# A WKV kernel: one row loaded by another engine's queue, six raw tiles in another pool, fewer leading zero matmuls

## Chip, cores and metric

The kernel runs on one core of a Trainium2 chip. The metric is the device time of one execution in microseconds (us), the median of several runs. A profile of one execution goes with it; its times are counted from the start of its span.

Names: PE is TensorE (matmuls; PEld its weight loads), DVE is VectorE, ACT is ScalarE, POOL is GpSimd, SP is SyncE. A "q" behind an engine's name stands for its sequencer, which issues DMAs and waits on semaphores.

## Reference

Inputs are w and u of 256 channels, and k and v of 16 sequences x 2048 steps x 256 channels, all float32. For each sequence and channel the reference runs along t with a weighted sum aa, its weight bb and a running maximum pp that keeps the exponentials in range:

```
ww = u + kk;  qq = max(pp, ww);  e1 = exp(pp - qq);  e2 = exp(ww - qq)
out[t] = (e1 * aa + e2 * vv) / (e1 * bb + e2 + 1e-08)
ww = pp - w + kk;  qq = max(ww, kk);  e1 = exp(ww - qq);  e2 = exp(kk - qq)
aa = e1 * aa + e2 * vv;  bb = e1 * bb + e2;  pp = qq
```

k, v and the output are 33.6 MB each.

## The kernel before, in words

Time is cut into 16 chunks of 128 steps (TC), the 16 sequences into 4 groups of 4. A step n = 4c + p is chunk c and group p, 64 steps in all (NP). A tile of k or v for a step is 128 x 4 x 256 float32, 512 KB: 128 time steps on the partitions, four sequences beside each other.

For a step n, in order:

- LK and LV load k and v (`load_k`, L104, `load_v`, L112). For n < 3 (BYSP) SP issues them, otherwise POOL.
- RK (`round_k`, L191) casts the raw k to fp32r on DVE or POOL. For some steps, 3 to 10 among them, the DMA casts on its way and there is no RK.
- R and L (`rows`, L196, and `logs`, L203), for q = 0 and 1, are the matmuls that make an exponent tile X in PSUM: R spreads the rows of w and u, which lie in the tile WU, over the time steps (L200), L adds sums of k over time (L206). There are two X tiles in turn.
- X (`exps`, L208) is ACT's exponential of an X tile into the ring EZR.
- CV casts v to bf16 (L213), TV multiplies it by the exponentials (L218, DVE).
- S (`sums`, L237) adds up over a chunk (L244). After four steps the state of the chunk is carried on by a chain of small operations on DVE, ACT and PE (`copy_sums` to `copy_back`, L248 to L306; L257 and L301 are its matmuls).
- Ten steps later (LAG) follow DEN, LN, INV, NUM, MUL and ST: denominators and numerators by PE (L321), logarithm and exponential by ACT (L329, L337), the product by DVE (L349) into an output tile of the pool opool, and the stores by SP, some of the last ones by POOL (L355, L362).

The order on all engines is written out by a planner. Each operation has a place (a number from the table P, by step), and the planner takes the first one in order of place whose predecessors are done and whose buffer is free (`free`, L370; NV = 4 raw tiles of vpool, NOT = 8 of opool). So buffers set the order of instructions, and on the chip an instruction that writes a buffer waits until the one before has been read. Each engine and each DMA queue works in its own order.

Zero matmuls on the tile Z (`zeros`, L146 to L148) fill PE's stream at fixed places: 38 at the very start, 12 before the rows of each of the first two X tiles (P["Z0"]["R"]), others later. They compute nothing that is used.

What comes before the first step: the tile WUf is cleared by DVE (L123). ACT issues the loads of w and u into it (`row_wu`, L120), one row of 256 channels each to four partitions. `make_rows` (L173, place "wu") turns it into WU on DVE (L174, L175) after DVE has cast the first k. POOL makes masks by selects (L83) and counts by iotas (L155), out of which DVE makes NLE, NLZ and CO (L159 to L163).

The first three k and v, raw, take tiles of vpool in the order k0, k1, v0, k2, v1, v2, then come v3 and the later v. vpool has four tiles, so v1, v2 and v3 wait until k0, k1 and k2 have been cast. The output tiles of opool are first needed when step 0 is finished.

Of the kernel before, what the change touches and what calls it, by code (L numbers as in the profile page):

```python
# [15 lines left out]
def kernel(  # L16
# [9 lines left out]
    K = tc.keep_in_program_order  # L26
    PE, DVE, SC, POOL, SP = nc.tensor, nc.vector, nc.scalar, nc.gpsimd, nc.sync
# [6 lines left out]
    NP = 4 * NST  # L34
    RING = 11
    LAG = 10.0
    SOON = 0
    UNTIL = 16
    SHARE = 0.2
    BYSP = 3  # L40
# [4 lines left out]
    CAP = 54.0  # L45
    BIG = 1e30
    FIRST = "DDDCCCCCCCC"
    VOT = 0
    XT = 8
    BYPOOL = 52  # L50
    BYQ = "PSSP"
# [16 lines left out]
    kppool = ctx.enter_context(tc.tile_pool(name="kppool", bufs=NKP))  # L68
    vpool = ctx.enter_context(tc.tile_pool(name="vpool", bufs=NV))
    vbpool = ctx.enter_context(tc.tile_pool(name="vbpool", bufs=NVB))  # L70
    rpool = ctx.enter_context(tc.tile_pool(name="rpool", bufs=NRD))
    opool = ctx.enter_context(tc.tile_pool(name="opool", bufs=NOT))
# [19 lines left out]
    def rows_of(x, n):  # L92
        c, p = divmod(n, 4)
        return x[4 * p:4 * p + 4, c * TC:(c + 1) * TC, :].rearrange("n t d -> t n d")

    KR, VR, VB = {}, {}, {}

    def how(n):
        return "D" if n < BYSP else FIRST[n] if n < len(FIRST) else PLAN[n % len(PLAN)]

    def raw(pool, tag):
        return pool.tile([128, 4, Dm], F32, tag=tag, name=tag)

    def load_k(n):  # L104
        if how(n) != "C":
            KR[n] = raw(vpool, "vr") if n < BYSP else raw(kppool, "kf")
            K((SP if n < BYSP else POOL).dma_start(out=KR[n], in_=rows_of(k, n)))  # L107
        else:
            KR[n] = kpool.tile([128, 4, Dm], F32R, tag="kr", name="kr")
            K(POOL.dma_start(out=KR[n], in_=rows_of(k, n)))  # L110

    def load_v(n):  # L112
        vr = raw(opool, "ot") if n < VOT else raw(vpool, "vr")
        K((SP if n < BYSP else POOL).dma_start(out=vr, in_=rows_of(v, n)))  # L114
        VR[n] = vr
# [4 lines left out]
    def row_wu(queue, x, g):  # L120
        K(queue.dma_start(out=WUf[g::32, :], in_=bass.AP(tensor=x.tensor, offset=x.offset, ap=[[0, 4], list(x.ap[0])])))

    K(DVE.memset(WUf, 0.0))  # L123
    load_k(0)
    row_wu(SC, w, 0)
    row_wu(SC, u, 1)
    K(SC.preload_act_table_set("natural_log_exp_and_others"))
    M1, I1 = matrix("M1", F32), matrix("I1", F32)
    K(DVE.memset(M1, -1.0))
# [16 lines left out]
    def zeros(m, first=False):  # L146
        for j in range(m):
            K(PE.matmul(TURN[:, 0:192], Z[:, 0:128], Z, start=first, stop=True, skip_group_check=True))  # L148

    zeros(38, True)  # L150

    select(M1, GE, 0.0, -1, -1, [[1, 128]])
    select(I1, NE, 1.0, 0, -1, [[1, 128]])
# [155 lines left out]
    RD, NUM, OT = {}, {}, {}  # L309
# [29 lines left out]
    def by_x(n):  # L339
        return n >= NP - XT and n % 2 == 1  # L340
# [16 lines left out]
    def shared(n):  # L357
        return n >= BYPOOL or BYQ[n % len(BYQ)] == "P" and n >= BYF
# [11 lines left out]
    ops, free = {}, {"K": NK, "KP": NKP, "V": NV, "N": 1, "RD": NRD, "OT": NOT, "VB": NVB}  # L370

    def step(name, place, fn, args=(), after=(), take=None, give=(), mode=0):
        key = name if isinstance(name, str) else " ".join(map(str, name))
        ops[name] = dict(place=AT.get(key, place), fn=fn, args=args, after=list(after), take=take, give=give, mode=mode)

    for n in range(NP):
        c, j = divmod(n, 4)
        early = n < BYSP
        vb = "OT" if n < VOT else "V"
        put = lambda key: n + P[key][j]  # L380
        lead = SOON * max(0.0, 1 - n / UNTIL)
        m = n + LAG - lead
        tail = n >= NP - LAG
        place = lambda key: m + (P["TAIL"][key] + (n - NP + LAG) * P["TAIL"]["step"] if tail else P["OUT"][key][j])
        kb = "V" if early else "KP" if how(n) != "C" else "K"
        if n:
            step(("LK", n), n + P["LK"], load_k, (n,), [("LK", n - 1)], kb)
        else:
            free["V"] -= 1
        step(("LV", n), n + P["LV"], load_v, (n,), [("LV", n - 1)] + ([("LK", n)] if n else []), vb)  # L390
        if how(n) != "C":
            step(("RK", n), put("RK"), round_k, (n,), [("LK", n), ("RK", n - 1)], "K", [kb])
        for q in range(2):
            step(("R", q, n), n + P["R"][q], rows, (n, q), ["wu", ("R", 1 - q, n - 1 + q)], "X", mode=3)
            step(("L", q, n), n + P["L"][q], logs, (n, q), [("R", q, n), ("LK", n), ("RK", n), ("L", 1 - q, n - 1 + q)], None,
                 ["K"] if q else [], 1)
            step(("X", q, n), n + P["X"][q], exps, (n, q), [("L", q, n), ("NUM", n - RING), ("S", n - RING)], None, ["X"])
        step(("CV", n), put("CV"), cast_v, (n,), [("LV", n), ("CV", n - 1)], "VB", [vb])
        step(("TV", n), put("TV"), times_v, (n,), [("X", 1, n), ("CV", n), ("TV", n - 1)], None, ["VB"])
        step(("S", n), put("S"), sums, (n,), [("TV", n), ("S", n - 1)] + ([("CS", c - 1)] if j == 0 else []), mode=2)  # L400
        if j == 3:
            s = P["STATE"][0 if c == 0 else 2 if c == NST - 1 else 1]
            for i, (name, fn, *after) in enumerate((
                    ("CS", copy_sums, ("S", n)), ("TU", turn, ("CS", c), ("CH", c - 1)), ("SL", state_logs, ("TU", c)),
                    ("FR", state_frames, ("SL", c), ("SN", c - 1)), ("OF", state_offsets, ("FR", c)),
                    ("SW", state_weights, ("OF", c)), ("CH", state_chain, ("SW", c), ("KP", c - 1)),
                    ("SS", state_spread, ("CH", c)), ("TK", turn_back, ("SS", c), "mats"), ("BK", copy_back, ("TK", c)),
                    ("SN", state_next, ("OF", c)), ("KP", state_keep, ("CH", c)))):
                if not (name in ("SN", "KP") and c + 1 == NST):
                    step((name, c), n + s[i] - lead * SHARE, fn, (c,), after, mode=1)  # L410
        step(("DEN", n), place("DEN"), den, (n,), [("BK", c), ("DEN", n - 1), "mats"], "X", mode=3)
        step(("LN", n), place("LN"), log_den, (n,), [("DEN", n), ("INV", n - 1)], "RD", ["X"])
        step(("INV", n), place("INV"), inverse, (n,), [("LN", n)])
        step(("NUM", n), place("NUM"), num, (n,), [("BK", c), ("TV", n), ("NUM", n - 1), "mats"], "X" if by_x(n) else "N", mode=3)
        step(("MUL", n), place("MUL"), mult, (n,), [("NUM", n), ("INV", n), ("MUL", n - 1)], "OT", ["X" if by_x(n) else "N", "RD"])
        step(("ST", n), place("ST"), store, (n,), [("MUL", n), ("ST", n - 1)], None, [] if shared(n) else ["OT"])
        if shared(n):
            step(("SQ", n), place("SQ"), store_rest, (n,), [("ST", n)], None, ["OT"])
# [6 lines left out]
    while todo:  # L425
# [15 lines left out]
        for g in o["give"]:  # L441
            if g == "X":
                x = held[("DEN", name[1]) if name[0] == "LN" else ("NUM", name[1]) if name[0] == "MUL" else ("R",) + name[1:]]
# [39 lines left out]
```

## Time and profile before

| | us |
|---|---|
| runs shown, median (lowest to highest) | 292.77 (292.13 to 294.27) |
| the profiled execution, its own time | 293.15 |
| its span | 291.4 |
| PE busy, TensorE's matmuls | 273.7 (94%) |
| ACT busy | 258.4 (89%) |
| DVE busy | 247.1 (85%) |
| POOL busy | 175.7 (60%) |
| DMA, HBM read and written | 345 GB/s over the span |

The granted TensorE clock over the profiled execution is 0.992 of full speed.

How to read it: a line of the timeline is start, length, engine, line of the kernel, operation, tile written <- tiles read, shapes, count, and in brackets the idle time of that engine before it and who ended it. A line of the chain of waits is start, length and what the chain passes through; "DMA" there lasts from the issue until the landing is signalled. A line of the windows query is a stretch, its length, the busy time of the engines in it (with the number of instructions), the granted clock, the DMA share and GB/s. The slices are fortieths of the span, in tenths of busy time.

### The profile page before, as it was taken

Reading aid. Unit: us, or ns where it says so; the run is one execution under the profiler, and the core shown is the slowest. Engines: PE = TensorE matmul, PEld = TensorE weight load, DVE = VectorE, ACT = ScalarE, POOL = GpSimd, SP = SyncE. Lnnn points to the kernel's source line nnn. Section 1 sums busy time; section 2 is a strip of 40 time slices with the busy share of each in tenths; the row PEclk is TensorE's granted clock in tenths of the full one; section 3 lists DMA queues with packets and bytes.
Section 4 is the critical chain, followed back from the end, with each engine's and each line's share of the span. In section 5 each row is a group of like instructions: output and inputs, shape, how many; then the busy total and the mean of one; then the engine's idle time right before and its main releaser. Section 6 shows DMA issues by size and latency. Waiting matters only on the chain.

```text
span 291.4 us, 8084 instructions
## 1 busy us (share of the span) xinstructions
PE 273.7 (94%) x3275; PEld 140.6 (48%) x3275; DVE 247.1 (85%) x423; ACT 258.4 (89%) x290; POOL 175.7 (60%) x218
## 2 busy tenths in 40 slices
PE   7999999999999999999999999999999999997750
PEld 7545744454545545444545455444545444544330
DVE  6575769989897989989898989899898989797860
ACT  1486398999999999999999999999999999997890
POOL 6177349575767687575767686675757674422230
PEclk9999999999999999999999999999999999999996
DMA  7999999999999999999999999999999999965885
GB/s 220 348 279 351 346 350 291 377 377 390 378 400 381 389 392 373 392 368 398 382 390 389 394 390 379 394 374 391 367 394 373 390 387 393 315 189 165 243 248 143
DMA packets 58550, 101.21 MB, mean 347 GB/s; under 512 B 5128, under 2 KB 43536, under 8 KB 58512
## 3 DMA queue, kind: packets, MB, share of 16 engines
q0 software_dynamic: 21216, 65.54, 65.0%
q1 hardware_dynamic: 37280, 35.14, 35.9%
q8 instruction: 25, 0.41, 0.6%
q14 instruction: 13, 0.11, 0.1%
q10 hardware_dynamic: 16, 0.01, 0.0%
HBM read 67.12 MB, written 33.55 MB: 345 GB/s over the span
## 4 chain that ended last, share of the span: by engine, by line
PE 71%; DMA 7%; DVE 5%; issue 5%; POOL 5%; ACT 4%; POOLq 0%; SPq 0%; ACTq 0%; DVEq 0%
PE X L206 17%; PE X L321 15%; PE num L321 12%; PE X L200 10%; PE TURN L148 9%; PE TOT L244 6%; DMA kf<-in_k_dram 4%; POOL vr L114 2%; DMA WUf<-in_u_dram 2%; PE TOT L257 2%; DVE ot L349 2%; POOL kr L110 2%; ACT EZR L209 1%; ACT rd L329 1%; DVE EZR L218 1%
## 5 line engine op out<-in xcount | busy, mean ns | idle before, releaser
L209 ACT ACTIVATE EZR<-X 128x1024 bf16<-128x1024 f32 x128 | 126.8, 1014 | 14.7 <-PE X L206 14.6
L213 POOL CAST vb<-vr 128x1024 bf16<-128x1024 f32 x54 | 56.3, 1043 | 70.9 <-DVE EZR L218 68.1
L218 DVE TENSOR_TENSOR EZR<-EZR,vb 128x2048 bf16<-128x2048 bf16 x64 | 77.9, 1219 | 0.4 <-ACT EZR L209 0.2
L349 DVE TENSOR_TENSOR ot<-num,rd 128x1024 f32<-128x1024 f32 x60 | 73.2, 1221 | 4.5 <-ACT rd L337 3.2
L337 ACT ACTIVATE rd<-rd 128x1024 f32<-128x1024 f32 (+1 forms) x65 | 67.9, 1046 | 2.0
L329 ACT ACTIVATE rd<-X 128x1024 f32<-128x1024 f32 x64 | 65.6, 1025 | 3.2 <-PE X L321 1.6
L148 PE MATMUL TURN<-Z 128*128 128x192 bf16 x331 | 57.0, 262 | 1.6 <-DVE Z L132 1.6
L114 POOL DMA_DIRECT2D vr<-in_v_dram x61 | 46.2, 758 | 13.8 <-DVE kr L193 7.1
L148 PEld LDWEIGHTS <-Z 128*128 128x128 bf16 x331 | 30.1, 102 | 49.0 <-issue 47.1
L200 PE MATMUL X<-WU,CO 64*64 64x512 bf16 x512 | 51.9, 390 | 0.9 <-DVE WU L175 0.6
L206 PE MATMUL X<-kr,NLE 128*128 128x512 f32 x128 | 45.6, 438 | 0.0
L206 PE MATMUL X<-kr,NLZ 128*128 128x512 f32 x128 | 45.5, 437 | 0.0
L107 POOL DMA_DIRECT2D kf<-in_k_dram x53 | 40.2, 758 | 0.0
L193 DVE CAST kr<-kf 128x1024 fp32r<-128x1024 f32 x39 | 31.9, 845 | 5.5 <-DMA kf<-in_k_dram 5.3
L200 PEld LDWEIGHTS <-CO 64*64 64x64 bf16 x512 | 15.7, 105 | 31.1 <-issue 26.2
L321 PE MATMUL X<-EZR,S 64*64 64x512 bf16 x256 | 26.2, 394 | 1.7 <-ACT rd L329 1.0
L321 PE MATMUL X<-cb,Id 64*64 64x512 bf16 x256 | 25.8, 376 | 0.0
L321 PE MATMUL X<-EZR,Id 64*64 64x512 bf16 x256 | 25.8, 376 | 0.0
L321 PE MATMUL num<-EZR,SN 64*64 64x512 bf16 x240 | 24.3, 386 | 1.5 <-DVE ot L349 1.5
L244 PE MATMUL TOT<-EZR,OH 128*32 128x256 bf16 x512 | 23.7, 277 | 0.7 <-DVE EZR L218 0.7
L321 PE MATMUL num<-cb,IdN 64*64 64x512 bf16 x240 | 24.0, 376 | 0.0
L321 PE MATMUL num<-EZR,IdN 64*64 64x512 bf16 x240 | 23.9, 376 | 0.0
(67 smaller groups left out, 268.9 us busy)
## 6 DMA issues: line engine op xcount, KB each, us to landing
vr<-in_v_dram POOLq DMA_DIRECT2D x61, 512.0 KB, 7.6
kf<-in_k_dram POOLq DMA_DIRECT2D x53, 512.0 KB, 8.5
out_dram<-ot SPq DMA_DIRECT2D x64, 256.0 KB, 9.1
out_dram<-ot SPq DMA_DIRECT2D x116, 128.0 KB, 9.7
kr<-in_k_dram POOLq DMA_DIRECT2D x8, 512.0 KB, 7.7
vr<-in_k_dram SPq DMA_DIRECT2D x3, 512.0 KB, 5.2
vr<-in_v_dram SPq DMA_DIRECT2D x3, 512.0 KB, 6.1
out_dram<-ot POOLq DMA_DIRECT2D x12, 128.0 KB, 3.1
```

What stands on the lines that cost most here:

```text
L114: K((SP if n < BYSP else POOL).dma_start(out=vr, in_=rows_of(v, n)))
L148: K(PE.matmul(TURN[:, 0:192], Z[:, 0:128], Z, start=first, stop=True, skip_group_check=True))
L200: K(PE.matmul(X[a][o:o + HS, i, :].rearrange("p (n d) -> p n d", n=2), CO[r:r + HS, q, :], WU[r:r + HS, :].unsqueeze(1).broadcast_to([HS, ...
L206: K(PE.matmul(X[a][:, i, :], (NLE, NLZ)[q], km[:, i, :], start=False, stop=True, skip_group_check=True))
L209: K(SC.activation(ez(n)[:, q, 1], X[a], ACT.Exp))
L213: K((DVE if n < EARLY else POOL).tensor_copy(vb, VR.pop(n)))
L218: K(DVE.tensor_mul(ez(n)[:, :, 0], ez(n)[:, :, 1], vb.unsqueeze(1).broadcast_to([128, 2, 2, D])))
L244: K(PE.matmul(t[32 * j:32 * j + 32, 0:256], OH[:, s:s + 32], ez(n)[:, 0, 1 - q, i, 256 * x:256 * x + 256], start=p == 0 and x == 0, stop=p ...
L321: K(PE.matmul(out_tile[o:o + HS, i, :], left, right, start=s == 0, stop=s == 2, tile_position=(r, o), skip_group_check=True))
L329: K(SC.activation(rd, X[a], ACT.Ln, scale=RS))
L337: K(SC.activation(RD[n][:, i], RD[n][:, i], ACT.Exp, scale=-1.0))
L349: K(DVE.tensor_mul(o.rearrange("p (i n) d -> p i (n d)", i=2)[:, i], NUM[n][:, i], RD[n][:, i]))
```

## The change

Three edits, and a line that is rewritten beside them:

- The load of u's row is issued by POOL, as its first instruction of the kernel, and no longer by ACT behind w's.
- The first three raw k and raw v are put in tiles of opool (8 tiles) and no longer of vpool (4 tiles). The six fit at once.
- 26 leading zero matmuls, not 38. The 12 before each of the first two rows stay.
- The places of the output operations are looked up by another index, and there is a list LAGS, which is empty.

```diff
+    LAGS = []
...
-    VOT = 0
+    VOT = 3
...
     def load_k(n):
         if how(n) != "C":
-            KR[n] = raw(vpool, "vr") if n < BYSP else raw(kppool, "kf")
+            KR[n] = raw(opool, "ot") if n < BYSP else raw(kppool, "kf")
...
     K(DVE.memset(WUf, 0.0))
     load_k(0)
+    row_wu(POOL, u, 1)
     row_wu(SC, w, 0)
-    row_wu(SC, u, 1)
...
-    zeros(38, True)
+    zeros(26, True)
...
-        m = n + LAG - lead
+        lag = LAG - sum(n < x for x in LAGS)
+        m = n + lag - lead
         tail = n >= NP - LAG
-        place = lambda key: m + (P["TAIL"][key] + (n - NP + LAG) * P["TAIL"]["step"] if tail else P["OUT"][key][j])
-        kb = "V" if early else "KP" if how(n) != "C" else "K"
+        place = lambda key: m + (P["TAIL"][key] + (n - NP + LAG) * P["TAIL"]["step"] if tail else P["OUT"][key][int(n + lag + 2) % 4])
+        kb = "OT" if early else "KP" if how(n) != "C" else "K"
...
-            free["V"] -= 1
+            free["OT"] -= 1
```

`load_v` is unchanged: it takes a tile of opool for n < VOT.

## The prediction, made before the run

> **What bounds the kernel now.** I read the page first, engines and slices, and then only the first 50 us, because the diff touches nothing later.
>
> ```profile
> PE 273.7 (94%) x3275; PEld 140.6 (48%) x3275; DVE 247.1 (85%) x423; ACT 258.4 (89%) x290; POOL 175.7 (60%) x218
> ...
> PE   7999999999999999999999999999999999997750
> ```
>
> TensorE is the bound: its row is 9s from slice 2 to slice 36. The windows query says how tight: 39.94 of 40 us busy from 80 to 120 us, and in all 6.6 us of gaps over 20 ns between its first and its last matmul, 4.9 of them after 258 us. What the change can give is therefore an earlier start of this stream, plus the few gaps inside it that a DMA causes. The chain of waits in order of time shows what sets the start:
>
> ```profile
> 2.35 5.60 DMA WUf<-in_u_dram
> 7.96 0.03 issue
> ...
> 8.05 0.30 DVE WU L174
> 8.36 0.03 issue
> 8.38 0.49 DVE WU L175
> 8.87 0.04 issue
> 8.92 0.41 PE X L200 x4
> ```
>
> The row of u, 4 KB, is issued second by ScalarE at 2.35 and has landed at 7.96. VectorE then makes WU, and the first real matmuls (L200) start at 8.92. The timeline shows how long each side waited:
>
> ```profile
> 1.41 0.29 POOL L83 TENSOR_SCALAR_AFFINE_SELECT M<-M 128x128 f32<-128x128 f32 x1 [0.90 <-DVE M L129]
> ...
> 1.64 6.68 PE L148 MATMUL TURN<-Z 128*128 128x192 bf16 x50 [1.64 <-DVE Z L132]
> ...
> 1.92 1.07 POOL L155 IOTA COf<- 1x128 f32 x4
> ...
> 3.18 0.27 DVE L163 CAST CO<-COf 128x128 bf16<-128x128 f32 x1
> ...
> 5.50 1.00 DVE L193 CAST kr<-vr 128x1024 fp32r<-128x1024 f32 x1
> ...
> 8.05 0.29 DVE L174 CAST WU<-WUf 128x256 bf16<-128x256 f32 x1 [1.55 <-DMA WUf<-in_u_dram]
> ...
> 8.92 0.41 PE L200 MATMUL X<-WU,CO 64*64 64x512 bf16 x4 [0.59 <-DVE WU L175]
> ...
> 13.07 0.75 POOL L114 DMA_DIRECT2D vr<-in_v_dram x1 [7.08 <-DVE kr L193]
> ```
>
> Three things: VectorE stood idle 1.55 us for u; TensorE's 50 zero matmuls (38 leading, 12 before the first rows) end at 8.33; GpSimd stood 7.08 us before it could issue v3, whose tile was k2's. That last wait shows as a hole in the transfers:
>
> ```profile
> 3.00:15.00 12.00, 11.32 (x90) 8.19 (x88) 7.47 (x28) 4.96 (x5) 4.13 (x10) 1.00 1.26 350
> 15.00:18.00 3.00, 2.82 (x22) 1.27 (x20) 2.14 (x3) 2.84 (x4) 2.96 (x4) 1.00 0.73 178
> 18.00:45.00 27.00, 27.00 (x279) 15.54 (x279) 18.53 (x32) 18.61 (x21) 14.45 (x19) 1.00 1.27 345
> ```
>
> The last column is GB/s: 178 in 15 to 18 us against 345 to 350 on both sides, so 3 x (1 - 178/348) = 1.5 us of transfer are lost.
>
> **The change part by part.** Everything is reckoned from the profiled execution: 293.15 us, span 291.4. It lies 0.38 above the median 292.77, and a saving is taken off both alike. The order of instructions on every engine is otherwise the same: LAGS is empty, and with LAG 10 the new index int(n+12)%4 is n%4, so that line moves nothing.
>
> *Row of u on GpSimd.* ScalarE issues one DMA less (0.51 us, hidden: its first exponential is at 10.05). GpSimd issues one more, ahead of its selects, once WUf is cleared (1.20), so from about 1.24. Its price isn't in the trace: GpSimd's store pieces (128 rows) take 0.60, its first load (512 rows) 0.91. Four rows are nearest to the smaller; as a first DMA may cost more, I take 0.65, and bound by 0.55 and 1.10 (ScalarE's first). The selects then start at about 1.95 to 2.0 in place of 1.41, the four iotas end 0.55 later, at 3.54, and CO (3.18, about 0.13 after it could have started) moves by some 0.42; all behind it on VectorE moves too. So the cast of k0 runs 5.92 to 6.92, and k3 and k4, issued by GpSimd at 4.32 and 5.22, go out 0.55 later, which costs nothing: k3 landed at 11.01 and its matmuls are at 16.77.
>
> Does u land by 6.92? Of w, issued at 1.23 on ScalarE, the packets moved from 4.74 to 4.98 us; u's, issued 1.12 later, from 7.03 to 7.25, and its signal came 0.71 after. For u at 1.24 the near row is w: landed 5.7. The other end is GpSimd's own first load, 6.69 us from issue to landing: 7.93, no gain. That load is 128 times the size and waited behind three others, so I take 5.7 to 6.5. VectorE is then the last, not the DMA: L174 starts at 6.95 instead of 8.05, 1.10 earlier.
>
> *Collision.* GpSimd's three issues (k3, k4 and now v3 at once) would run from 4.87 to 7.3, under Id, the k0 cast and L174. In the trace one of two such neighbours is stretched: the k0 cast under an issue took 1.00 against 0.69 for the others, and the issues at 14.55 and 15.60 took 1.06 and 1.12 against 0.75. Half of it lies under the k0 cast already; L174 and L175 are newly exposed, 0 to 0.6; I take 0.2. First rows: 8.92 - 1.10 + 0.20 = 8.0, a gain of 0.9 (0.0 to 1.4).
> The Trainium skill, "SBUF — State Buffer", section "SBUF: two separate sides", says that a VectorE instruction in a 2-port mode, such as an fp32 copy, keeps GpSimd from writing descriptors until it ends. [...]
>
> *26 zeros instead of 38.* The zeros start 160 ns apart until 6.58 us and 82.5 ns apart after (32 in the first 4.94 us). Of 38, 32 are slow and 6 fast: the last ends at 7.34 instead of 8.33. It had to go, or TensorE would hold the rows at 8.33; with it TensorE idles about 0.65 before them, against 0.59 now. Gain by itself nothing.
>
> *Raw tiles of the outputs.* v1 and v2 are issued by SP at about 2.9 and 3.4 instead of 6.53 and 9.50, and v3 right behind k4. The ninth transfer then lands at about 17 instead of 18.52, and the loads behind it, limited by bandwidth until 43 us, come 1 to 2 us earlier. v1 and v2 now move ahead of k3 and k4: at 1.5 us for each 512 KB k3 lands at 14.0 and k4 at 15.5 at the latest; wanted are they at 15.9 and 18.9. No output needs these tiles before 46.5 us. What it gives on TensorE is small: the gap at 46.43 (0.24, behind VectorE's 2.35 us wait for a k), and perhaps the 0.38 at 238.0, behind another such wait of 1.27. The other waits for transfers on VectorE (0.41, 1.05 and 0.81 before 29 us) end in no TensorE gap. I take 0.3 (0 to 0.6).
>
> Sum: 0.9 + 0.3 = 1.2. 293.15 - 1.2 = 291.95 for such an execution, 292.77 - 1.2 = 291.6 for the median.
>
> **The rivals.** B, GpSimd's start is the new bound. If the issue can't end before VectorE's first memsets do (2.15), it ends at 2.15 + 0.60 = 2.75, the selects move 1.37, CO 1.24, the k0 cast ends at 7.75, L174 starts there: gain 0.3, or 0.1 with the collision, plus 0.3 on the loads: 292.4. For it: the stretched rows. Against it: selects and iotas ran beside the same memsets at their usual lengths.
> C, u lands no earlier (7.93 as worked out): the start stands still, the loads give 0.3: 292.5. Then the change doesn't do what it says.
> D, all goes well: rows right after the zeros (7.34, gain 1.58) and both DMA gaps gone (0.62): 2.2, so 290.6.
> E, slower: the zeros also prepare TensorE's pace. If the idle time ahead of the rows makes it fall back to 160 ns, an X tile's rows and logs take 1.02 x 160/82.5 = 1.98, against the pace of now of 1.10 a tile (rows start seven times from 10.95 to 17.57), for as long as the first slow stretch, 4.94 us: 2.5 tiles done instead of 4.5, a loss of 2.2 and with the gain of 1.2 a net +1.0: 293.8. It decides once the idle time is enough for the fall; the 0.59 now was not, and I expect 0.65.
> The Trainium skill, "TensorE: Matmul & The Clock Gate", part 1, puts the fall at an idle window of about 3.4 us, free-running; the step at 6.58 is the same thing seen rising, and by that rule E needs far more idle time.
>
> **How the numbers follow.** Forecast 0.60 (own range 290.7 to 292.3), B 0.14, C 0.10, D 0.09, E 0.05 and 0.02 for other shifts in the long full stretch. The predicted time is that of the forecast, 291.6. The range takes in D below and B and C above, with the scatter of the runs (292.13 to 294.27): 290.1 to 293.4. One per cent is 2.9 us, about what a measurement here can tell from no change. No sum above reaches it: faster by more 0.04, slower by more 0.03, the rest 0.93.
>
> **What would show it.** L174's wait for u gone, L174 near 7.0 and the first rows near 8.0 right or wrong for the start; CO's start near 3.6 for GpSimd's price; no 7 us wait ahead of v3 and no hole at 15 to 18 us for the tiles; a smaller wait at 43 us. If the rows start earlier and the end doesn't move, the later stream is not bound by TensorE as I read it. Zeros still 160 ns apart after 8.5 us would be E.

## The result, and the profile after

| | before | after |
|---|---|---|
| median (lowest to highest), 16 runs each | 292.47 us (291.75 to 294.27) | 291.51 us (290.85 to 292.24) |
| the profiled execution, and its span | 293.15, 291.4 us | 291.05, 289.3 us |

The ratio of the runs is 0.9956, 95% interval 0.9944 to 0.9969: 1.3 us faster (0.9 to 1.6). The two medians themselves lie 0.96 us apart. Two later readings of the same kernel gave 0.9977 (0.9962 to 0.9992) and 0.9969 (0.9954 to 0.9983). The two profiled executions lie 2.1 us apart: more than the medians, because the one before was one of the slower and the one after one of the faster of its kind.

The chain of waits after no longer passes through the landing of u. It now passes through GpSimd's issue of that row and what GpSimd does behind it (the line numbers are higher by one):

```profile
1.50 0.10 POOL WUf L122
1.61 0.65 issue
...
2.35 0.32 POOL M L84
...
3.72 0.24 POOL COf L156
3.97 0.02 issue
3.99 0.23 DVE CO L164
...
6.30 0.60 DVE kr L194
6.90 0.41 DVE WU L175
7.31 0.03 issue
7.33 0.49 DVE WU L176
7.83 0.04 issue
7.87 0.41 PE X L201 x4
```

The first rows start at 7.87 instead of 8.92. The timeline shows what each engine waited for:

```profile
1.50 0.75 POOL L122 DMA_DIRECT2D WUf<-in_u_dram  x1 [0.99 <-DVE I L131]
...
1.65 5.35 PE L149 MATMUL TURN<-Z 128*128 128x192 bf16 x38 [1.65 <-DVE Z L133]
...
2.69 0.29 DVE L160 TENSOR_SCALAR NLE<-M 128x128 fp32r<-128x128 f32 x1 [0.53 <-POOL M L84]
...
3.99 0.23 DVE L164 CAST CO<-COf 128x128 bf16<-128x128 f32 x1 [0.26 <-POOL COf L156]
...
6.22 0.68 DVE L194 CAST kr<-ot 128x1024 fp32r<-128x1024 f32 x1
6.83 0.47 DVE L175 CAST WU<-WUf 128x256 bf16<-128x256 f32 x1
...
7.20 0.77 POOL L115 DMA_DIRECT2D vr<-in_v_dram  x1
...
7.87 0.41 PE L201 MATMUL X<-WU,CO 64*64 64x512 bf16 x4 [0.88 <-DVE WU L176]
```

VectorE has two new short waits for GpSimd, 0.53 and 0.26 us, and has lost the 1.55 us wait for u. GpSimd issues v3 at 7.20 and no longer at 13.07. The windows query (a stretch, its length, engines, clock, DMA share, GB/s) shows the hole closed, 345 against 178 GB/s:

```profile
15.00:18.00 3.00, 2.91 (x27) 1.36 (x29) 2.21 (x4) 2.67 (x4) 1.94 (x4) 1.00 1.35 345
18.00:45.00 27.00, 27.00 (x281) 15.38 (x277) 19.69 (x36) 18.74 (x22) 15.86 (x20) 1.00 1.25 342
```

How far TensorE's stream is ahead can be read by setting the same matmul of both traces side by side: 1.05 us from the first rows to 45 us, 1.66 from 60 to 237 us, 2.02 from 250 us to the end. The second step, near 46 us, is the place where VectorE had waited for a k. Before, the sums (L244) were split by a wait; after, they run through. The timeline before, then after:

```profile
45.93 0.51 PE L244 MATMUL TOT<-EZR,OH 128*32 128x256 bf16 x10
...
46.67 0.40 PE L244 MATMUL TOT<-EZR,OH 128*32 128x256 bf16 x6 [0.24 <-DVE EZR L218]
46.67 0.11 PEld L244 LDWEIGHTS <-OH 128*32 128x32 bf16 x5 [0.52 <-issue]
```

```profile
40.80 1.16 DVE L194 CAST kr<-kf 128x1024 fp32r<-128x1024 f32 x1 [1.16 <-DMA kf<-in_k_dram]
...
44.88 0.62 PE L245 MATMUL TOT<-EZR,OH 128*32 128x256 bf16 x16
```

The gap that the profile gives for it was 0.24 us, but the weight loads stood still for 0.52: a matmul here lasts 0.27 from start to modelled end, and that hides as much of the wait. VectorE's wait for the k has shrunk from 2.35 to 1.16 us and no longer reaches TensorE.

It is not shown, though, that the change removed this gap. Of 14 profiles only that of the kernel before has it. Experiment 5 below has neither the early row nor the tiles, and its hole at 15 to 18 us is as deep (185 GB/s), yet its sums run through as well:

```profile
42.58 1.17 DVE L193 CAST kr<-kf 128x1024 fp32r<-128x1024 f32 x1 [1.78 <-DMA kf<-in_k_dram]
...
46.03 0.62 PE L244 MATMUL TOT<-EZR,OH 128*32 128x256 bf16 x16
```

Its stream goes from 0.10 us behind the kernel before to 0.48 ahead at this place, without the edits that would explain it. There the k landed at 42.56 instead of 43.03, and half a microsecond was enough. With the early row it lands at 40.8 to 41.2 and is needed 1.05 earlier, so the gap becomes less likely; how often an execution of the kernel before has it can't be told from its one profile.

The third step, 0.37 us at 238, doesn't belong to the change. Gaps of 0.36 to 0.44 ahead of a numerator stand in 10 of the 14 profiles, one or two in each, at 125, 139, 155, 157, 188, 189, 204, 237 and 238 us, with the tiles and without.

### The profile page after: what moved, and what is told of

The parts are those of the page before. It is cut to its first block, busy times and chain, and to the rows that moved or that the text cites. A ratio compares the mean times of both kernels' runs of the same rounds, so it can differ in the third digit from the quotient of the medians.

```text
span 289.3 us, 8057 instructions
## 1 busy us (share of the span) xinstructions
PE 272.0 (94%) x3263; PEld 139.5 (48%) x3263; DVE 246.1 (85%) x423; ACT 258.1 (89%) x290; POOL 176.9 (61%) x219
## 4 chain that ended last, share of the span: by engine, by line
PE 83%; DVE 4%; ACT 4%; issue 3%; POOL 1%; DMA 1%; POOLq 0%; SPq 0%; DVEq 0%
PE X L207 21%; PE X L322 15%; PE num L322 13%; PE X L201 12%; PE TURN L149 12%; PE TOT L245 7%; ACT EZR L210 2%; PE TOT L258 2%; DVE ot L350 1%; PE TURN L302 1%; POOL out_dram L356 1%; DMA out_dram<-ot 1%; ACT rd L330 1%; DVE EZR L219 1%; ACT rd L338 1%
## 5 line engine op out<-in xcount | busy, mean ns | idle before, releaser
L149 PE MATMUL TURN<-Z 128*128 128x192 bf16 x319 | 55.7, 261 | 1.6 <-DVE Z L133 1.6
L149 PEld LDWEIGHTS <-Z 128*128 128x128 bf16 x319 | 28.9, 101 | 48.9 <-issue 47.1
L194 DVE CAST kr<-kf 128x1024 fp32r<-128x1024 f32 x39 | 30.6, 813 | 4.4 <-DMA kf<-in_k_dram 4.2
```

## The experiments

The theory was that start and tiles are two terms, 1.05 us and 0.3 to 0.6 us. Several of the expectations below still take the second step for a gain of the edits. Rivals: one edit gives it all; the tiles give nothing, or cost something; idle time in front of the rows costs TensorE its pace. All ratios are against the kernel before on the same chip.

**1. Row of u alone.**

```diff
+    row_wu(POOL, u, 1)
     row_wu(SC, w, 0)
-    row_wu(SC, u, 1)
```

> The kernel before, with u's row issued by GpSimd as its first instruction and nothing else. By the prediction's sum the 50 zero matmuls now hold the rows: they end at 8.33 in the profile before and 38 + 12 of them still run, so the first rows come at 8.2 to 8.4 instead of 8.92, a start gain of 0.5 to 0.7 us, and the wait of 7 us ahead of v3 and the hole at 15 to 18 us stay. Time 0.5 us below the kernel before. Rival, all of the change's gain is the row of u: 1.2 us or more below. Rival, the row gives nothing without the tiles: 0.

Measured: 0.9950 (0.9928 to 0.9971), 1.5 us, more than expected. The rows start at 7.98, close on the zeros, which end at 8.05 in this execution; the hole is nearly gone without the tiles:

```profile
15.00:18.00 3.00, 2.91 (x24) 1.32 (x26) 1.83 (x2) 2.67 (x4) 1.64 (x3) 1.00 1.22 314
```

So the hole was for the most part a consequence of the late start: v2 and v3 wait for the casts of k1 and k2, the first of which stands behind the making of WU and the second behind the first step's matmuls. v2 is issued at 8.45 instead of 9.50, v3 at 12.13 instead of 13.07. The stream is 0.6 us further ahead behind 46 us here too, as in every profile but the one before.

**2. Row and 26 zeros, three times.** The edit above, and

```diff
-    zeros(38, True)
+    zeros(26, True)
```

> Row of u by GpSimd and 26 leading zero matmuls, raw tiles as before. If start and tiles are separate terms, the first rows stand where the whole change has them (7.87), 1.05 us earlier than before, the hole at 15 to 18 us stays and with it a TensorE gap near 46 us; time 1.0 us below the kernel before. Rival, the tiles give nothing on the median (the two profiled executions differ by 2.1 us, the medians by about 1.1): then this is as fast as the whole change, 1.0 to 1.3 below, and it can't be told from the first reading but by the gaps at 46 and 238 us in its profile.

> Row of u and 26 zeros without the tiles, the other half of the comparison: 1.3 to 1.7 us below the kernel before, and within 0.2 of the whole change if the tiles add nothing once the row is early.

> The other half of the third comparison: 1.3 to 1.6 us below the kernel before.

Measured: 0.9945 (0.9929 to 0.9962), 0.9955 (0.9938 to 0.9972) and 0.9957 (0.9938 to 0.9976), rows at 7.87 or 7.88. It is not 1.0 us below, as separate terms would have it, but 1.3 to 1.6, as much as the whole change or more. Nor can it be told from row alone: with the row early, no gain of the twelve zeros less is measured.

**3. Tiles alone.** The raw tiles in opool as in the change, u's row and the zeros as before.

> The first three raw k and v in tiles of the outputs, u issued by ScalarE second as before, 38 leading zero matmuls. The first rows stay at 8.9 (u is still what VectorE waits for), no hole at 15 to 18 us, VectorE's wait for a k near 43 us shorter, the TensorE gap at 46.4 us gone. By the prediction 0.3 us below the kernel before (0 to 0.6); by the profile of the whole change, where the stream gained 0.61 near 46 us and 0.37 near 238 us, up to 1.0. Rival, the tiles are worth nothing: 0 within 0.3.

Measured: 0.9987 (0.9968 to 1.0005), 0.4 us with an interval that holds 0. The rows stay at 8.96, the gap at 46.4 is gone, and the stream is 0.57 us ahead behind it in the profile; since experiment 5 shows 0.58 at this place without the tiles, that isn't evidence for them. Alone, the tiles close part of the hole (237 GB/s), and the k that VectorE waits for lands 1.2 us earlier (41.82). In experiments 6 and 7, which have the tiles but late matmuls, the hole is there (169 and 190 GB/s): with the tiles too it lasts until k5 can be issued, and that waits for step 1's matmuls (15.05 and 14.85 there, 13.49 in the change).

**4. The whole change, twice more, beside row and zeros.**

> The whole change again, beside row and zeros without the tiles, on the same chip. The profiles so far say that either edit closes the hole at 15 to 18 us: the stream was 1.05 us early until 46 us and 1.6 after with and without the tiles. Theory: start 1.05 plus 0.55 near 46 us, so 1.3 to 1.7 below the kernel before, and no more than 0.2 better than row and zeros. Rival, the tiles are a term of their own on top: 0.3 to 0.6 better than row and zeros. Rival, the tiles cost something (first readings 0.9956 with, 0.9945 without): 0.3 worse.

> The whole change, third reading, with row and zeros on the same chip. Readings so far: 0.9956 and 0.9977 with the tiles, 0.9945 and 0.9955 without. If the tiles cost something of their own, this is again 0.2 to 0.6 us slower than row and zeros; if that was scatter, the two differ by less than 0.2.

Measured: 0.9977 and 0.9969, beside 0.9955 and 0.9957 without the tiles. No gain of the tiles on top of the row is measured; the medians lie 0.4 and 0.5 us above those without them, in the same direction as in the first readings. The intervals overlap each time, and no profile shows a place for such a cost (the stream is 1.6 to 1.7 us ahead from 60 to 130 us in all six), so it remains open whether it is real.
A reading that fits: once the row is early, the loads behind the hole go by k5, the next one that GpSimd issues behind v3. It waits for step 1's matmuls in both kernels, goes out at 13.49, and lands at 19.75 with the tiles (the profile after) and at 19.86 without (the first row and zeros). The k that VectorE waits for near 41 us lands at 40.78 to 41.16 with them and at 40.79 to 41.08 without.

**5. 26 zeros alone.**

> 26 leading zero matmuls and nothing else. u lands at 8.0 as before, so the rows stay at 8.9; TensorE idles 1.3 to 2.1 us before them. By the prediction no change by itself (within 0.2). Rival E in its mild form: idle time of up to 2 us ahead of the rows already costs pace in some executions, 0.3 to 1 us slower with a lower granted clock.

Measured: 1.0027 (1.0003 to 1.0050), 0.8 us slower (0.1 to 1.5). Of the 12 runs eight lie at 292.45 to 293.79 us with a mean granted clock of 0.988 to 0.992; their median, 292.80, is that of the kernel before beside it (292.83). Four took 294.24 to 295.37 with 0.981 or 0.982. The profiled execution is one of the eight, 292.59 us with TensorE idle 2.23 us before the rows and no loss of pace. The four fit the mild form of rival E; no profile shows one of them.

**6. Eight leading zeros** in the whole change.

```diff
-    zeros(26, True)
+    zeros(8, True)
```

> The whole change with 8 leading zero matmuls and not 26. The zeros then end near 4.9 us and TensorE idles some 3.0 us before the rows, against 0.88. Rival E of the prediction, in a form where it should bite: if idle time ahead of the rows keeps or makes TensorE slow (160 ns a zero), the step to 82.5 ns comes only after 9 us, an X tile's rows and logs take up to 1.98 against 1.10, and the time is 1 to 2.5 us above the whole change, with a lower granted clock. If idle time of 3 us does not matter, the same as the whole change within 0.3.

Measured: 1.0025 (1.0013 to 1.0038), against 0.9977 for the whole change beside it, so 1.4 us above. The rows start at 7.87 as in the whole change, after 2.84 us of idle time, and the granted clock (the third number from the right) is 0.72 from 7 to 13 us:

```profile
0.00:7.00 7.00, 3.38 (x20) 2.95 (x21) 4.71 (x36) 1.28 (x1) 5.38 (x19) 1.00 0.73 222
7.00:13.00 6.00, 5.13 (x32) 2.96 (x32) 1.85 (x4) 1.44 (x2) 0.96 (x2) 0.72 1.18 345
13.00:16.00 3.00, 2.82 (x21) 1.31 (x20) 2.90 (x5) 2.84 (x4) 0.95 (x1) 1.00 1.32 355
```

Narrower stretches show a fall and a new rise, 3.41 us apart:

```profile
4.95:8.37 3.42, 0.58 (x7) 0.37 (x7) 3.38 (x15) 0.00 (x0) 3.01 (x5) 1.00 1.10 352
8.37:11.78 3.41, 3.41 (x19) 2.08 (x18) 0.10 (x1) 1.02 (x1) 0.00 (x0) 0.50 1.18 344
```

The zeros between the first rows and the second are 160 ns apart, from 9.33 to 10.93. At 46 us the stream is 1.56 us behind that of the whole change. So in this execution rival E's fall happened. Not all of the loss is explained by it: only seven of the 12 runs have a granted clock of 0.982 to 0.984, as the profiled one; the other five have 0.990 to 0.992 and are no faster (293.35 to 294.12 us against 292.27 to 293.57). The granted clock reads 1.00 over the first slow stretch in every profile here, so a rise that comes late would not lower it; whether that is what the five have, no profile shows.

**7. u's row behind the iotas.**

```diff
-    row_wu(POOL, u, 1)
...
     for g in range(0, 128, 32):
         K(POOL.iota(COf[g:g + 1, :, :], pattern=[[-1, 2], [1, HS]], base=-HS // 2, channel_multiplier=0,
                     allow_small_or_imprecise_dtypes=True))
+    row_wu(POOL, u, 1)
```

> The whole change, but GpSimd issues u's row behind its iotas (near 3.0 us) and not first (1.50), so that selects, iotas, NLE and CO stand where they were before. If GpSimd's own delay is what matters (rival B's mechanism), CO is back at 3.2, the k0 cast at 5.5, and the rows come earlier than 7.87. If the landing of u matters: it took 5.05 to 5.2 us from issue in the profiles so far, so u lands at 8.0 to 8.2, WU's cast waits for it as in the kernel before, the first rows come at 8.9 to 9.1, and the time is 1.0 to 1.2 us above the whole change, with the tiles' gain alone left (0.4 to 0.6 below the kernel before).

Measured: 1.0033 (1.0010 to 1.0057), against 0.9977 for the whole change beside it, so 1.6 us above, and 1.0 (0.3 to 1.7) above the kernel before, where 0.4 to 0.6 below was expected. GpSimd's selects and CO are back in their old places (CO at 3.18, the k0 cast at 5.21), but the row, issued at 2.94, lands 5.4 us later, and VectorE waits for it:

```profile
8.35 0.29 DVE L175 CAST WU<-WUf 128x256 bf16<-128x256 f32 x1 [2.46 <-DMA WUf<-in_u_dram]
...
9.21 0.41 PE L201 MATMUL X<-WU,CO 64*64 64x512 bf16 x4 [1.53 <-DVE WU L176]
```

The landing counts; GpSimd's 0.75 us at the front is the price of it. The start explains 1.34 us of the 1.6; the mean granted clock is 0.982 or 0.983 in four of the 12 runs (294.11 to 294.88 us), as in experiment 5. The tiles' gain that was to be left doesn't show.

**8. u's row by SP** behind k0, in the whole change.

```diff
-    row_wu(POOL, u, 1)
+    row_wu(SP, u, 1)
```

> The whole change, but u's row issued by SP right behind k0 and not by GpSimd. If GpSimd's longer start is what now sets VectorE's pace (in the profile after, NLE waits 0.53 us for a select and CO 0.26 us for the iotas), CO goes back to about 3.2, the k0 cast to 5.5, WU starts at 6.2 to 6.6 and the first rows come at 7.1 to 7.5 instead of 7.87: 0.4 to 0.7 us below the whole change, 1.5 below the kernel before. Rival, the landing of u itself limits (6.55 in the profile after, WU's cast at 6.83): if SP's row lands at 6.5 or later, the rows don't come before 7.4. Rival, the row in SP's queue delays k1, v0 and k2 by 0.5 us each and gives the gain back: same as the whole change.

Measured: median 297.34 us. The profiled execution took 292.62 with a granted clock of 0.988, the other five 295.80 to 298.28 with 0.977 to 0.982. The ratio of 1.0044 (0.9996 to 1.0093) rests on the two fastest of the six and decides nothing. In the profile the rows do start earlier, at 7.63. But k1 and all transfers behind it in SP's queue are 0.7 us later and v2 lands at 17.2 (14.3 in the whole change). VectorE's queue stands for v2, and TensorE for VectorE:

```profile
17.32 0.69 DVE L214 CAST vb<-ot 128x1024 bf16<-128x1024 f32 x1 [3.30 <-DMA ot<-in_v_dram]
...
17.57 0.50 PE L245 MATMUL TOT<-EZR,OH 128*32 128x256 bf16 x10
...
19.20 0.40 PE L245 MATMUL TOT<-EZR,OH 128*32 128x256 bf16 x6 [1.13 <-DVE EZR L219]
```

At that place the stream goes from 0.24 us ahead of the whole change to 1.17 behind it. What lowers the clock in the other five runs isn't in this profile.

**9. Cast of k0 on ScalarE**, with row and zeros and without the tiles.

```diff
-        K((DVE if how(n) == "D" else POOL).tensor_copy(kr, KR[n]))
+        if n < 1:
+            K(SC.activation(kr, KR[n], ACT.Copy))
+        else:
+            K((DVE if how(n) == "D" else POOL).tensor_copy(kr, KR[n]))
```

> Row and zeros, and the cast of k0 on ScalarE, which is idle until its first exponential at 9.0, instead of VectorE. If VectorE's queue and the landing of u (6.55 to 6.7) are nearly level in the change, taking the 0.68 us cast off VectorE leaves the landing as the last: WU's cast at 6.65 to 6.8 instead of 6.83 but without the cast's tail, and beside fewer neighbours; the first rows at 7.45 to 7.7, 0.2 to 0.4 us below row and zeros. Rival, VectorE's queue was the limit alone: WU's cast at 6.3, rows at 7.15, 0.7 below. Rival, ScalarE's cast is late (after k0's landing at 4.9 it takes about 1.0, to 6.0): no cost expected.

Measured: 0.9951 (0.9933 to 0.9969), beside 0.9957 for row and zeros: not to be told apart. The start behaves as expected, WU's cast waits 0.30 us for u and the rows come at 7.54:

```profile
6.61 0.35 DVE L174 CAST WU<-WUf 128x256 bf16<-128x256 f32 x1 [0.30 <-DMA WUf<-in_u_dram]
...
7.54 0.41 PE L203 MATMUL X<-WU,CO 64*64 64x512 bf16 x4 [0.41 <-DVE WU L175]
...
17.47 0.98 PE L247 MATMUL TOT<-EZR,OH 128*32 128x256 bf16 x16
```

The last line shows where it went: the sixteen sums take 0.98 us instead of 0.62, with no gap shown, because they wait for the product with v1, which stands behind the cast of v2. The lead falls from 1.38 to 1.04 there. With the tiles v2 lands at 14.3 us, here at 16.1; the two together were not run.

## Why the prediction was right, point by point

- *The bound.* Right. The end moved with TensorE's stream, whose lead, once gained, stays within 0.03 us from 60 to 237 us.
- *Row of u on GpSimd.* The mechanism is right, VectorE and not u being last; the parts were off in both directions. GpSimd started at 1.50 and not 1.24 and took 0.75 and not 0.65, so the k0 cast began at 6.22 and not 5.92. The 1.24 allowed 0.04 us behind the memset of WUf, which ended at 1.20. The trace before shows 0.30 for GpSimd: k2's cast ended at 12.77 and the issue of v3, which waited for it, began at 13.07. The profile puts the start at 1.50 down to the memset of I (ended at 1.49), which the row doesn't need; 1.20 + 0.30 gives 1.50 without it, and no run separates the two. The cast then took 0.68 and not 1.00; what was stretched beside GpSimd's issues was S (0.44 against 0.21) and WU's first cast (0.47 against 0.29). L174 began at 6.83 (6.95 forecast). u landed at 6.55, just past the 5.7 to 6.5: the distance to VectorE was 0.3 us, where the near row, w, had suggested more. Experiments 7 and 9 show that u's landing takes over as soon as either side moves.
  Rival B let u's issue wait for the memsets. The issue ran from 1.50 to 2.25 beside memsets of VectorE and took 0.75 us, as long as most of GpSimd's later loads (0.74 to 0.76), so no wait for memsets shows.
  The Trainium skill's "SBUF — State Buffer", "SBUF: two separate sides", says that a VectorE instruction with at most one SBUF input, outside the 2-port modes, does not contend with GpSimd. The memsets here agree with that.
- *Start*, 0.9 forecast: 1.05 measured.
- *26 zeros.* "It had to go, or TensorE would hold the rows at 8.33" is wrong as a rule: it took the step of the pace at 6.58 us as fixed. In 13 profiles the step from 160 to 82.5 ns lies at 4.50 to 7.37 us, so 50 zeros would end at about 7 to 9 us. Experiment 1 lost 0.1 us of its start to them (rows at 7.98, not 7.87), and no time that can be measured. "Gain by itself nothing" holds for eight of the 12 runs of experiment 5; with the other four it is a loss of 0.8 us (0.1 to 1.5).
- *Raw tiles*, 0.3 forecast: the step that failed. That the loads come 1 to 2 us earlier is right (the k that VectorE waits for lands at 41.82 with the tiles alone, 40.78 in the whole change, 43.03 before). That this is worth something to TensorE isn't shown: the gap at 46.43 from which the term was priced stands in one profile alone and is missing in experiment 5, which has no tiles. In time the tiles alone are 0.4 us with an interval that holds 0, and on top of the row they bring no gain (experiment 4). The prediction also read the hole as a lack of tiles; it follows the late rows, since the row alone nearly closes it (314 GB/s) and the tiles with late matmuls don't (169 and 190).
- *The sum*, 1.2 forecast, came to 1.3 (0.9 to 1.6) in the first reading and 0.7 and 0.9 in the two later ones. That it fits is in part luck: the start was taken 0.15 too small, and the 0.3 of the tiles is a term that no run shows. That 291.6 lies so near the 291.51 measured is in part luck too, as the kernel before had a median of 292.47 here and not 292.77. By their medians the three readings of the whole change gain 0.96, 0.91 and 0.88 us, close to the 1.05 of the start alone; those of row and zeros gain 1.60, 1.27 and 1.37, and what makes the rest there is open.
- *Rivals.* B is half true: GpSimd's start is on the chain and moves the k0 cast by 0.72 us. C's late landing is seen only in experiment 7 (8.3), where the row is issued 1.4 us later. D's start was bounded by VectorE, not by the zeros, which ended at 7.00. E's fall did not happen in the change: 0.88 us of idle time, and no execution of the whole change has a granted clock below 0.988. With 2.8 us it happened in the profile of experiment 6, and with some 2.2 us four of 12 runs fit it; that E needs far more idle time than the 0.65 forecast was right.
  By the Trainium skill, "TensorE: Matmul & The Clock Gate", part 1, the window is free-running and some 3.4 us long, and it must be busy for the pace to rise. The traces agree in part: fall and rise in experiment 6 lie 3.41 us apart, and the step's spread over 13 profiles, 2.9 us, is less than one such window. But the earliest step came 2.85 us after the first matmul, and the fall after a stretch of 3.42 us with 0.58 us of matmuls in it.

## What to carry to other kernels

When a gap of one profile is missing in the next, look at the profiles of kernels without the edit before the edit is credited with it: here the 0.6 us near 46 us was missing in all 13 others. Before two edits are added up, time them alone and together. A hole in the transfers can follow from an earlier wait; ask whether it would still be there after that one is closed. Filler that keeps an engine's pace is priced over the spread of its switching time, not by one profile; and a wait inside a run of matmuls is read from start to start, since the profile's modelled ends hid one matmul's length (0.27 us here) of it.

## What the runs showed of the hardware

- A row of 4 KB issued by GpSimd took 0.75 us to issue and 5.0 to 5.4 us to land, beside the bulk loads of SP. ScalarE's first took 1.11 to issue.
- The eight loads of GpSimd that waited for another engine in the first 40 us of the trace before began 0.29 or 0.30 us after it was done; u's row began 0.30 us after the memset of WUf.
- TensorE's first matmuls run at half pace (zeros 160 and not 82.5 ns apart) until a moment that differs by 2.9 us between executions of nearly the same program, while the granted clock in the records reads 1.00 for that stretch.
- After a stretch of 3.42 us in which TensorE worked 0.58 us, the granted clock fell to 0.50 for 3.41 us (experiment 6).
- With 26 leading zeros and late rows (2.23 us of idle time in the profiled execution) the mean granted clock was 0.981 or 0.982 in four of 12 runs and 0.988 to 0.992 in the others.
